# Gated stage of a two-layer hybrid trunk: low halves of weights and operand sums moved from GpSimd to VectorE

## The chip, the cores and the metric

The kernel runs on one core of a Trainium2 chip. The metric is the device time of one execution in microseconds; the median of the runs counts. Engines are named as in the profile: PE (TensorE, matrix products), PEld (its weight loads), DVE (VectorE), ACT (ScalarE), POOL (GpSimd), SP (SyncE, which issues most transfers).

## What is computed

Two layers of a trunk with three parallel branches, over 512 sample tokens and 128 prompt tokens, width 1024, all in fp32. A layer, cut to what matters here:

```python
h = rms_norm(x, norm_g) * (1 + scale) + shift
rq, rk, rv, rz, q_lat, kv_lat, k_r, mz, fu, fz, gl = split(h @ w_in)
o_r = retention(rq, rk, rv); o_m = latent_attention(...); o_f = fourier_mix(fu)
branches = stack([o_r * silu(rz), o_m * silu(mz), o_f * silu(fz)])      # three of width 512
proj = einsum('btnw,nwd->btnd', branches, w_branch)                     # 512 -> 1024 each
merged = sum(proj * sigmoid(gl.reshape(B, T, 3, 1024)), axis=2)
x = x + gate * (merged @ w_out)
```

The gated stage is the part from the last Fourier gates to `merged`: for each of the three branches a product of `h` with 1024 gate columns `gl`, a sigmoid, a product of the branch with its 512 x 1024 matrix, the elementwise product of both, and the sum over branches.

## The kernel before

Activations lie transposed: features on the 128 partitions, 640 tokens (512 + 128) along the free axis, one tile for each 128 features. fp32 products are made from two reduced-precision parts: a value is split into a high half (a cast by ScalarE, `ACT.copy` at L78) and a low half (`low`, L73 and L74: source minus high half, one two-input subtraction on the engine given as `leng`, VectorE by default). A product is then three matmuls, high x high, high x low, low x high (`mm3`, L84 to L87).

A layer runs attention, retention, Fourier mixing, the gated stage and the output projection in turn. In the gated stage every product of a 2 x 2 block structure is made with seven block products instead of eight (`seven`, L1045): the right operand's blocks and the weights' blocks are first summed in certain combinations, then seven products are accumulated in PSUM banks of 320 columns (`bank`, six of them), and each is folded into the two outputs by adds on VectorE that read PSUM (L1052). Per layer:

- 13 gate weight groups of 256 columns (`gl_weights`, L1010): two loads of 512 KB into two `raw` buffers (`wraw`, there are two in all), four sums of 512 columns on VectorE (`wsums`, L1004 to L1008), and splits. The tiles are w1 (1024 columns: the first raw tile as loaded), w2 (two halves of 512: the two sums), w4 (512), and w3 (1024: the first raw tile after the sums changed it in place). Casts of w1 and w3 are at L1015 and L1025. One group (columns `C_FZ + 256`) is for the Fourier gates, 12 are for the branches.
- 12 branch weight groups (`br_weights`, L1031): one load of 512 KB, four sums of 256 columns, and splits of 512, 256, 512 and 512 columns.
- 3 sets of operand sums (`branch_sums`, L975): for each branch seven operand blocks of 2 x 320 columns are split, and four blocks are formed by subtraction or addition.

A raw buffer can be loaded again when its last reader is done; so the casts and low halves that read it, on ScalarE, GpSimd and VectorE, set when the SP queue can issue the next load.

The loop at L1169 goes over the branches (indices 1, 0, 2), and in each over eight steps: an even step makes the gates of 256 columns (`gl_weights`, `seven`), an odd step the branch product (`br_weights`, `seven`), multiplies both (L1203, two inputs, 640 columns) and, from the second branch on, adds the result to the sum `mg` (L1205, 640 columns). The operand sums of the second and third branch are interleaved with the first gate products of that branch. Between the products, matrix products of the conditioning vector (`mod`, L173) are poured in: 12 blocks in layer 0, four in layer 1.

The program is built with a tile framework that inserts the semaphores and plans the order of the instructions on each engine by a timeline of its own (`schedule_with_timeline_sim=True`, L1361); within an engine instructions then run in that fixed order. The order therefore need not be the order of the source: the sums of a branch weight group stand between the PSUM adds of the gate products before it.

In the gated stage before the change the low halves are shared out by hand. In `gl_weights` VectorE makes the first half of w1 and the second sum's half of w2; GpSimd makes the second half of w1, the first sum's half of w2, w4, and w3 in two instructions. In `br_weights` VectorE makes one of 512 columns, GpSimd two of 512 and one of 256. In `branch_sums` GpSimd makes four of seven low halves and one of four sums. Of each two additions at L1205 GpSimd makes one.

Of the kernel before, what the change touches and what calls it, by code (L numbers as in the profile page):

```python
# [11 lines left out]
ALU = mybir.AluOpType  # L12
# [18 lines left out]
def build(nc, tc, A, O):  # L31
    ACT, DVE, POOL, PE = nc.scalar, nc.vector, nc.gpsimd, nc.tensor
# [40 lines left out]
    def low(eng, hi, lo, src):  # L73
        eng.tensor_tensor(lo, src, hi.bitcast(F32), op=ALU.subtract)  # L74

    def split(hi, lo, src, scale=None, leng=DVE):
        if scale is None:
            ACT.copy(hi, src)  # L78
            low(leng, hi, lo, src)
        else:  # L80
            ACT.mul(hi, src, scale)
            DVE.scalar_tensor_tensor(lo, src, scale, hi.bitcast(F32), op0=ALU.mult, op1=ALU.subtract)
# [24 lines left out]
    def rows(w, k0, nk, c0, n):  # L107
        return w[k0 * P:(k0 + nk) * P, c0:c0 + n].rearrange("(k p) n -> p k n", p=P)

# [1 line left out]
    ident = cp.tile([P, P], F32, name="ident")  # L111
    make_identity(nc, ident)
    ones = cp.tile([P, 1], F32, name="ones")
# [20 lines left out]
    vT = cp.tile([P, P], F32, name="vT")  # L134
    DVE.tensor_copy(vT, vps[:, :P])

    # silu of the conditioning vectors
    cs = cp.tile([P, 2 * NK + 30], F32, name="cs")
    DVE.memset(cs, 0.0)
    cth = cp.tile([P, 2, NK], F32, name="cth")  # L140
# [1 line left out]
    DVE.scalar_tensor_tensor(cth, cth, 1.0, cT, op0=ALU.add, op1=ALU.mult)  # L142
    DVE.tensor_scalar(cs[:, 0:2 * NK].rearrange("p (k c) -> p k c", c=2), cth.rearrange("p c k -> p k c"), 0.5, None, op0=ALU.mult)

    # log sigmoid of the decay logits
    ab = cp.tile([P, 16], F32, name="ab")
    DVE.scalar_tensor_tensor(ab, lg, -1.0, lg, op0=ALU.mult, op1=ALU.max)
    ey = cp.tile([P, 16], F32, name="ey")
# [168 lines left out]
                self.pour(24)  # L317
            return self.done[n - 1]

# [1 line left out]
    def lat_mm(acc, t, k, wh, wl, kk):  # L321
        ts_ = slice(t * P, (t + 1) * P)
        return mm3(acc, hh[k][:, ts_], hl[k][:, ts_], wh[:, kk, :], wl[:, kk, :], k == 0, k == NK - 1)
# [4 lines left out]
    def attention(l, ap, w, acc):  # L328
# [35 lines left out]
        for t in order:  # L364
# [2 lines left out]
                lat_mm(a, t, k, *w[k // 3], k % 3)  # L367
            ACT.copy(latv[t], a)
            inv_rms(t, 1, latv[t][:, 0:256], 256)
        # queries  # L370
        wq = []
        for k in range(3):
            rv = wraw(A["w_q_up"][l, k * P:(k + 1) * P, :].unsqueeze(1), 1, 768)
            hi, lo = wtiles(1, 768)
# [24 lines left out]
        mz = Filler(l, [C_MZ + P * w for w in range(4)])  # L399
        mz.finish(1)  # L400

        # keys: normalised latents and rotary parts, both transposed
        nc.sync.dma_start(gkv, A["kv_norm_g"][l].partition_broadcast(P))
        ckh = ap.tile([P, 2, KEYS], F32R, name="ckh")
        ckl = ap.tile([P, 2, KEYS], F32R, name="ckl")
# [28 lines left out]
            POOL.tensor_copy(kth[i][64:96, :], kth[0][64:96, :])  # L434
            POOL.tensor_copy(ktl[i][64:96, :], ktl[0][64:96, :])

        # key/value up-projection weights, nope and value columns apart
        wkv = []
        for k in range(2):
            rv = wraw(A["w_kv_up"][l, k * P:(k + 1) * P, :].unsqueeze(1), 1, 1024)  # L440
            hi, lo = wtiles(1, 1024)
            s = rv.rearrange("p a (h two e) -> p (a two) h e", two=2, e=64)
# [193 lines left out]
                DVE.tensor_tensor(bv[:, :, r], sv[:, :, r], sinv[:, r].unsqueeze(1).to_broadcast([P, nh, 2, 8]), op=ALU.mult)  # L636
        DVE.tensor_tensor(out, a[:, :nh], b[:, :nh], op=ALU.add)

# [1 line left out]
    def retention(l, rp, orr, spare):  # L640
        pos = rp.tile([P, 2, T], F32, name="pos")
        nc.sync.dma_start(pos, A["k_pos"].partition_broadcast(P))
# [169 lines left out]
        norm(3)  # L812
        gate(3)

# [1 line left out]
    def fourier(l, fp, of, sums):  # L816
        def table(name, src, a, n):
            raw = fp.tile([P, a, n], F32, name="traw", tag="traw", bufs=1)
# [111 lines left out]
    def fourier_gate(of, g, z):  # L930
        DVE.scalar_tensor_tensor(of[g], of[g], 0.5, z, op0=ALU.mult, op1=ALU.mult)

# [1 line left out]
    HALF = (slice(0, 320), slice(320, 640))  # L934

    def resplit(hi, lo, eng):
# [38 lines left out]
    def branch_sums(gp, src, spare):  # L975
        sv = src.rearrange("p (i k) n -> p i k n", i=2)
        B = lambda i, c: sv[:, i, :, HALF[c]]
        t = [gp.tile([P, 2, 320], F32R, name=f"bq{i}", tag=f"bq{i}", bufs=1) for i in range(10)]
        x = [spare[:, i, :].rearrange("p (k n) -> p k n", k=2) for i in range(4)]
        t = t[:8] + x[:2] + t[8:] + x[2:]  # L980

        def place(i, x, eng):
            hi, lo = t[2 * i:2 * i + 2]
            split(hi, lo, x, leng=eng)
            return [(hi[:, k, :], lo[:, k, :]) for k in range(2)]

        def run():
            p0 = place(0, B(0, 0), POOL)
            p5 = place(5, B(1, 1), DVE)
            yield p0  # L990
            POOL.tensor_tensor(B(1, 1), B(1, 1), B(0, 1), op=ALU.subtract)
            DVE.tensor_tensor(B(0, 1), B(0, 1), B(0, 0), op=ALU.subtract)
            DVE.tensor_tensor(B(0, 0), B(0, 0), B(1, 1), op=ALU.add)
            yield place(1, B(0, 0), DVE)
            yield place(2, B(1, 0), POOL)
            DVE.tensor_tensor(B(1, 0), B(1, 0), B(0, 0), op=ALU.subtract)
            yield place(3, B(0, 1), DVE)
            yield place(4, B(1, 1), POOL)
            yield p5
            yield place(6, B(1, 0), POOL)  # L1000

        return run()

# [6 lines left out]
    def gl_weights(gp, l, c0):  # L1010
        r1 = wraw(rows(A["w_in"][l], 0, NK, c0, P), NK, P)
        r2 = wraw(rows(A["w_in"][l], 0, NK, c0 + P, P), NK, P)
        lo, up = slice(0, 4), slice(4, 8)
        w1, w2 = wtiles(NK, P), wtiles(NK, P)
        ACT.copy(w1[0], r1)  # L1015
        low(DVE, w1[0][:, lo], w1[1][:, lo], r1[:, lo])
        low(POOL, w1[0][:, up], w1[1][:, up], r1[:, up])
        s1, s2 = (gp.tile([P, 4, P], F32, name="st", tag="st", bufs=2) for _ in range(2))
        wsums(r1[:, lo], r1[:, up], r2[:, lo], r2[:, up], s1, s2)
        split(w2[0][:, up], w2[1][:, up], s2, leng=DVE)  # L1020
        split(w2[0][:, lo], w2[1][:, lo], s1, leng=POOL)
        w4 = [gp.tile([P, 4, P], F32R, name=f"w4{i}", tag=f"w4{i}", bufs=1) for i in range(2)]
        split(w4[0], w4[1], r2[:, up], leng=POOL)
        w3 = wtiles(NK, P)
        ACT.copy(w3[0], r1)  # L1025
        low(POOL, w3[0][:, lo], w3[1][:, lo], r1[:, lo])
        low(POOL, w3[0][:, up], w3[1][:, up], r1[:, up])
        g = lambda w, s: (w[0][:, s], w[1][:, s])
        return g(w1, lo), g(w2, up), g(w1, up), g(w2, lo), g(w3, lo), g(w3, up), w4

    def br_weights(gp, l, idx, c0):  # L1031
        r = wraw(rows(A["w_branch"][l, idx], 0, 4, c0, 256), 4, 256)
        w1, w2 = wtiles(NK, P), wtiles(NK, P)
        c1, c2 = slice(0, P), slice(P, 256)
        s = [slice(2 * i, 2 * i + 2) for i in range(4)]
        split(w1[0][:, 0:4], w1[1][:, 0:4], r[:, :, c1], leng=POOL)
        split(w2[0][:, s[2]], w2[1][:, s[2]], r[:, 2:4, c2], leng=POOL)
        st = gp.tile([P, 4, P], F32, name="st", tag="st", bufs=2)
        wsums(r[:, 0:2, c1], r[:, 2:4, c1], r[:, 0:2, c2], r[:, 2:4, c2], st[:, 0:2], st[:, 2:4])
        split(w1[0][:, 4:8], w1[1][:, 4:8], st, leng=POOL)  # L1040
        split(w2[0][:, 0:4], w2[1][:, 0:4], r[:, :, c1], leng=DVE)
        g = lambda w, i: (w[0][:, s[i]], w[1][:, s[i]])
        return g(w1, 0), g(w1, 3), g(w1, 1), g(w1, 2), g(w2, 0), g(w2, 1), g(w2, 2)
# [23 lines left out]
                add(y2[:, a], y2[:, a])  # L1067
            yield i

# [1 line left out]
    first = []  # L1071

    po1 = sm()
# [45 lines left out]
    for l in range(DEPTH):  # L1119
# [25 lines left out]
        with ExitStack() as s:  # L1145
# [4 lines left out]
            blocks = [(0, b) for b in range(8, 12)] + [(1, b) for b in range(8)] if l == 0 else [(1, b) for b in range(8, 12)]  # L1150
# [18 lines left out]
            for n, (idx, src, tmp) in enumerate(((1, omt, None), (0, ort, om), (2, ort, om))):  # L1169
                parts = branch_sums(gp, src, bql)  # L1170
                bq = [] if n else list(parts)
                for step in range(8):
# [25 lines left out]
                    for st in seven(br_weights(gp, l, idx, 256 * i), bq, *ps):  # L1198
                        if st in (3, 6):
                            next(steps, None)  # L1200
                        if st in (5, 6):
                            y, m, p = y2[st - 5], ms[st - 5], ps[st - 5]
                            DVE.scalar_tensor_tensor(p, y, 1.0, p, op0=ALU.add, op1=ALU.mult)  # L1203
                            if n:
                                (POOL if st == 5 else DVE).tensor_tensor(m, m, p, op=ALU.add)  # L1205
            merge(NK)
        s3.close()
        oft = rp2.tile([P, 4, TT], F32, name="xb", tag="of", bufs=1)
# [156 lines left out]
```

## Time and profile before

| | |
|---|---|
| median of the three runs | 1592.85 us (1592.19 to 1600.37) |
| the profiled execution, span from first to last instruction | 1591.8 us |
| mean granted PE clock | 0.975 |
| gated stage of layer 0, of layer 1 (from the table of windows) | about 442 to 752 us, 1212 to 1516 us |
| busy in the whole span: PE, DVE, ACT, POOL | 1470.8, 1174.7, 740.0, 647.4 us |
| chain that ended last: PE, DVE, issue, DMA, ACT, POOL | 53, 25, 10, 5, 4, 2% |

How to read the rows. In a table of windows each row is one stretch of time: its length, the busy time of each engine with the number of its instructions, the mean granted clock of PE, the share of the DMA engines and GB/s. In a row of the view by source line the three numbers behind the count are the shortest, median and longest duration in ns, then when the first and the last one started, then the shapes. In a view of groups the numbers are the busy time of all, the mean of one, and the idle time of the engine just before them with what ended it. In the timeline a row is start, duration, engine, line, operation, output <- inputs. In the view of waits the three numbers are the time in all, how often, and the longest. L74 is the subtraction that makes a low half, whoever asks for it; the tile names (wl, w, bq, bql) tell them apart. Busy time includes time in which an instruction has begun and is held up.

### The profile page before, as it was taken

How to read it: one execution, taken by the hardware profiler on the slowest of the kernel's cores; microseconds unless marked ns; L12 is line 12 of the kernel's file. 1: busy time of each engine (PE TensorE's matmuls, PEld its weight loads, DVE VectorE, ACT ScalarE, POOL GpSimd, SP SyncE). 2: the span in 40 equal slices, each digit the busy share in tenths (PEclk: the TensorE clock that was granted, in tenths of full speed). 3: DMA queues.
4: the chain of work that ended last, by engine and by line, in shares of the span. 5: the costliest groups of instructions: out<-in, count | busy, mean ns of one | idle time of the engine just before them, and what ended most of it. 6: DMA issues, size and time to landing. Idle time of an engine off the chain costs nothing.

```text
span 1591.8 us, 25637 instructions
## 1 busy us (share of the span) xinstructions
PE 1470.8 (92%) x9713; PEld 1358.5 (85%) x9713; DVE 1174.7 (74%) x1974; ACT 740.0 (46%) x1563; POOL 647.4 (41%) x485
## 2 busy tenths in 40 slices
PE   5999999999889989899999999999988998987997
PEld 3989999979888877788999899998888887887887
DVE  5267775466899899999564777555598899899953
ACT  5456666354444433434254676644344434334332
POOL 1220004444465656665311101164364656575550
PEclk9999999999999999999999999999999999998999
DMA  9320004221134443334532000332122442222342
GB/s 338 121 70 6 10 17 135 74 68 41 48 111 113 121 139 106 93 106 137 159 90 83 15 15 14 100 92 72 37 54 64 136 125 88 67 67 66 84 130 79
DMA packets 174250, 138.93 MB, mean 87 GB/s; under 512 B 8752, under 2 KB 165040, under 8 KB 174128
## 3 DMA queue, kind: packets, MB, share of 16 engines
q1 hardware_dynamic: 172976, 136.94, 29.4%
q8 instruction: 76, 1.25, 0.3%
q10 hardware_dynamic: 1152, 0.37, 0.1%
q14 instruction: 46, 0.38, 0.1%
HBM read 125.98 MB, written 11.30 MB: 86 GB/s over the span
## 4 chain that ended last, share of the span: by engine, by line
PE 53%; DVE 25%; issue 10%; DMA 5%; ACT 4%; POOL 2%; SPq 0%; POOLq 0%; DVEq 0%; ACTq 0%
PE sm L85 5%; PE sm L87 5%; PE sm L86 5%; PE bank L85 4%; PE bank L87 4%; PE bank L86 4%; PE big L491 4%; PE fill L302 3%; PE sm L302 3%; DMA raw<-in_w_in 3%; PE big L253 2%; PE sm L512 2%; DVE wl L74 2%; DVE om L1052 2%; DVE raw L1008 2%
## 5 line engine op out<-in xcount | busy, mean ns | idle before, releaser
L74 POOL TENSOR_TENSOR wl<-raw,wh 128x512 fp32r<-128x512 f32 (+2 forms) x172 | 288.1, 1688 | 456.4 <-ACT wh L78 268.7
L78 ACT CAST wh<-raw 128x512 fp32r<-128x512 f32 (+4 forms) x142 | 109.6, 774 | 170.4 <-DVE raw L1008 56.1
L85 PE MATMUL sm<-wh,hh 128*128 128x256 f32 (+2 forms) x456 | 134.0, 295 | 4.7 <-DVE vl L74 2.3
L85 PE MATMUL bank<-hh,wh 128*128 128x320 f32 x416 | 132.8, 319 | 5.2 <-DVE om L1052 4.5
L87 PE MATMUL sm<-wh,hl 128*128 128x256 f32 (+2 forms) x456 | 132.9, 293 | 2.3 <-DVE hl L74 2.3
L86 PE MATMUL sm<-wl,hh 128*128 128x256 f32 (+2 forms) x456 | 133.3, 292 | 0.0
L86 PE MATMUL bank<-hl,wh 128*128 128x320 f32 x416 | 131.6, 316 | 0.0
L87 PE MATMUL bank<-hh,wl 128*128 128x320 f32 x416 | 130.3, 313 | 0.0
L74 POOL TENSOR_TENSOR wl<-st,wh 128x512 fp32r<-128x512 f32 x50 | 78.3, 1567 | 104.0 <-ACT wh L78 98.9
L78 ACT CAST wh<-st 128x512 fp32r<-128x512 f32 x76 | 47.0, 619 | 158.2 <-DVE st L1005 103.0
L85 PE MATMUL bank<-bq,wh 128*128 128x320 f32 x240 | 80.7, 337 | 16.4 <-ACT om L1054 7.6
L85 PEld LDWEIGHTS sm<-wh,hh 128*128 128x128 f32 x456 | 87.0, 191 | 6.5 <-DVE vl L74 2.7
L74 DVE TENSOR_TENSOR wl<-raw,wh 128x512 fp32r<-128x512 f32 (+4 forms) x74 | 82.2, 1116 | 14.0 <-ACT wh L78 14.0
L85 PEld LDWEIGHTS bank<-hh,wh 128*128 128x128 f32 x416 | 80.0, 192 | 12.9 <-DVE om L1052 8.6
L87 PEld LDWEIGHTS sm<-wh,hl 128*128 128x128 f32 x456 | 86.9, 191 | 3.1 <-DVE hl L74 2.6
L86 PEld LDWEIGHTS sm<-wl,hh 128*128 128x128 f32 x456 | 87.1, 191 | 0.5 <-issue 0.4
L86 PE MATMUL bank<-bq,wh 128*128 128x320 f32 x240 | 78.1, 326 | 8.5 <-DVE bq L74 8.5
L86 PEld LDWEIGHTS bank<-hl,wh 128*128 128x128 f32 x416 | 80.2, 193 | 0.0
L87 PEld LDWEIGHTS bank<-hh,wl 128*128 128x128 f32 x416 | 80.0, 192 | 0.0
L1052 DVE TENSOR_TENSOR om<-bank,om 128x320 f32<-128x320 f32 x168 | 76.7, 481 | 3.5
L74 DVE TENSOR_TENSOR ptl<-sm,pth 128x384 fp32r<-128x384 f32 x128 | 67.3, 549 | 14.1 <-ACT pth L78 13.1
L87 PE MATMUL bank<-bq,wl 128*128 128x320 f32 x240 | 77.6, 323 | 0.0
(571 smaller groups left out, 4945.9 us busy)
## 6 DMA issues: line engine op xcount, KB each, us to landing
raw<-in_w_in SPq DMA_DIRECT2D x96, 512.0 KB, 4.0
mraw<-in_w_mod SPq DMA_DIRECT2D x64, 256.0 KB, 3.9
raw<-in_w_branch SPq DMA_DIRECT2D x24, 512.0 KB, 3.4
raw<-in_w_out SPq DMA_DIRECT2D x16, 512.0 KB, 4.3
mraw<-in_w_mod SPq DMA_DIRECT2D x4, 1024.0 KB, 11.7
mraw<-in_w_mod SPq DMA_DIRECT2D x8, 512.0 KB, 7.9
raw<-in_w_in SPq DMA_DIRECT2D x8, 384.0 KB, 4.5
om<-xd SPq DMA_DIRECT2D x16, 192.0 KB, 3.1
```

Of the source, the lines that this page charges most:

```text
L74: eng.tensor_tensor(lo, src, hi.bitcast(F32), op=ALU.subtract)
L78: ACT.copy(hi, src)
L85: PE.matmul(out, ah, bh, start=first, stop=False)
L86: PE.matmul(out, ah, bl, start=False, stop=False)
L87: return PE.matmul(out, al, bh, start=False, stop=last)
L253: PE.matmul(ps[:, 512 * h:512 * h + 320], ws[a][:, k, :], xs[b][k][:, 320 * h:320 * h + 320], start=(first and k == 0 and i == 0), stop=(l ...
L302: PE.matmul(ps, w[a][:, k, :], (hh, hl)[b][k][:, hs], start=(k == 0 and i == 0), stop=(k == NK - 1 and i == 2))
L491: PE.matmul(S[:, 512 * h:512 * h + 384], qT[hd][a][:, t * P:(t + 1) * P], (kth, ktl)[b][hd % 3][:, 384 * h:384 * h + 384], start=(i == 0), ...
L512: PE.matmul(po[:, :256], vt[hd // 4][kt][:, hd % 4, :], pts[hd, qb][b][kt // 3][:, kt % 3, :], start=(kt == 0 and b == 0), stop=(kt == 5 a ...
L1008: DVE.tensor_tensor(a12, a12, s2, op=ALU.subtract)
L1052: add = lambda o, v: DVE.tensor_tensor(o, ps, v, op=ALU.add)
```

## The change

Low halves and sums of the gated stage move from GpSimd to VectorE, and where a tile's low half was made in two instructions it becomes one:

```diff
 branch_sums:
-            p0 = place(0, B(0, 0), POOL)
+            p0 = place(0, B(0, 0), DVE)
...
-            POOL.tensor_tensor(B(1, 1), B(1, 1), B(0, 1), op=ALU.subtract)
+            DVE.tensor_tensor(B(1, 1), B(1, 1), B(0, 1), op=ALU.subtract)
...
-            yield place(2, B(1, 0), POOL)
+            yield place(2, B(1, 0), DVE)
...
-            yield place(4, B(1, 1), POOL)
+            yield place(4, B(1, 1), DVE)
...
-            yield place(6, B(1, 0), POOL)
+            yield place(6, B(1, 0), DVE)
 gl_weights:
         ACT.copy(w1[0], r1)
-        low(DVE, w1[0][:, lo], w1[1][:, lo], r1[:, lo])
-        low(POOL, w1[0][:, up], w1[1][:, up], r1[:, up])
+        low(DVE, w1[0], w1[1], r1)
...
         ACT.copy(w3[0], r1)
-        low(POOL, w3[0][:, lo], w3[1][:, lo], r1[:, lo])
-        low(POOL, w3[0][:, up], w3[1][:, up], r1[:, up])
+        low(DVE, w3[0], w3[1], r1)
 br_weights:
-        split(w2[0][:, s[2]], w2[1][:, s[2]], r[:, 2:4, c2], leng=POOL)
+        split(w2[0][:, s[2]], w2[1][:, s[2]], r[:, 2:4, c2])
...
-        split(w1[0][:, 4:8], w1[1][:, 4:8], st, leng=POOL)
+        split(w1[0][:, 4:8], w1[1][:, 4:8], st)
 the loop over the branches:
-                                (POOL if st == 5 else DVE).tensor_tensor(m, m, p, op=ALU.add)
+                                DVE.tensor_tensor(m, m, p, op=ALU.add)
```

GpSimd keeps, in `gl_weights`, the low halves of the first sum (part of w2) and of w4, 512 columns each, and in `br_weights` that of the first 512 columns of w1. `hidden_sums` (L940 to L973), which runs in the Fourier stage and uses GpSimd, is not touched. The rest of the diff replaces comment lines by empty ones.

## The prediction

> **What bounds the kernel now.** I read the page first, then the table of windows over the two gated stages, then the same table cut at the places where one weight group follows the next.
>
> ```profile
> PE 1470.8 (92%) x9713; PEld 1358.5 (85%) x9713; DVE 1174.7 (74%) x1974; ACT 740.0 (46%) x1563; POOL 647.4 (41%) x485
> ```
>
> ```profile
> core 0: us, PE busy (x) PEld busy (x) DVE busy (x) ACT busy (x) POOL busy (x), PEclk, DMA share, GB/s
> 442.00:752.00 310.00, 284.66 (x1836) 250.23 (x1834) 284.25 (x387) 120.74 (x201) 185.48 (x121) 0.98 0.40 115
> 1212.00:1516.00 304.00, 269.31 (x1680) 252.19 (x1679) 281.57 (x374) 117.23 (x192) 181.84 (x121) 0.94 0.32 89
> ```
>
> Over the whole program the matrix engine is the bound. In the gated stages (one per layer, together 614 of 1591.8 us) VectorE is as full as PE: 284.25 of 310 us and 281.57 of 304. So the question is which of the two comes last, and where. The next rows cut the stages into pairs: one gate weight group with its seven products, then one branch weight group with its seven.
>
> ```profile
> 521.00:542.60 21.60, 21.60 (x146) 19.37 (x146) 19.27 (x28) 8.30 (x14) 11.23 (x8) 1.00 0.44 124
> 542.60:572.00 29.40, 25.84 (x170) 22.29 (x169) 28.79 (x35) 12.58 (x21) 21.57 (x13) 1.00 0.36 100
> 572.00:594.80 22.80, 22.07 (x145) 19.32 (x146) 20.64 (x31) 8.10 (x14) 13.36 (x9) 1.00 0.55 166
> 594.80:619.10 24.30, 22.38 (x148) 19.39 (x147) 21.31 (x30) 8.19 (x14) 13.78 (x9) 1.00 0.40 114
> 619.10:642.60 23.50, 21.68 (x133) 18.16 (x131) 21.11 (x30) 8.20 (x14) 13.76 (x9) 0.93 0.37 102
> 642.60:673.80 31.20, 26.60 (x166) 23.51 (x165) 30.67 (x36) 12.68 (x21) 23.45 (x14) 0.94 0.33 94
> 673.80:697.10 23.30, 23.30 (x149) 20.34 (x148) 20.62 (x31) 8.11 (x14) 13.28 (x9) 0.93 0.37 105
> 697.10:722.20 25.10, 22.89 (x151) 19.91 (x150) 21.84 (x30) 8.20 (x14) 13.28 (x9) 1.00 0.38 110
> 1314.70:1344.40 29.70, 24.93 (x156) 22.97 (x155) 29.16 (x36) 12.58 (x21) 21.54 (x13) 0.91 0.25 68
> 1367.20:1390.00 22.80, 20.39 (x118) 19.76 (x119) 21.16 (x29) 7.82 (x13) 13.35 (x9) 0.85 0.26 70
> 1390.00:1412.80 22.80, 20.76 (x136) 19.64 (x134) 21.32 (x28) 7.83 (x13) 13.42 (x9) 1.00 0.25 70
> 1412.80:1442.80 30.00, 21.59 (x121) 20.47 (x120) 29.58 (x35) 12.69 (x21) 21.33 (x14) 0.86 0.20 54
> ```
>
> Three kinds of window show. In pairs of the first branch (521.0) PE is busy for 21.60 of 21.60 us at full clock: nothing that frees VectorE shortens them. In pairs of the second and third branch (594.8, 697.1, 1390.0) PE has gaps or a lowered clock, and VectorE is busy all but 1.5 to 3 us. At the change from one branch to the next (542.6, 642.6, 1314.7, 1412.8; I call them transitions) VectorE is full, 29.58 of 30.00, and PE waits. So the change can act in the second and third kind: 12 plain pairs, four transitions, and the two entries of the stages.
>
> **What VectorE's time is made of.** Its busy time is not all work. These rows give smallest, median and largest duration of one instruction in ns, and below them a stretch of both engines' instructions in order of time.
>
> ```profile
> L1052 DVE TENSOR_TENSOR om<-bank,om x168: 472/478/493, 562.3 to 1520.5; 128x320 f32<-128x320 f32 x168
> L1203 DVE SCALAR_TENSOR_TENSOR om<-tg,om x16: 812/1868/2850, 606.0 to 1521.1; 128x640 f32<-128x640 f32 x16
> L74 DVE TENSOR_TENSOR wl<-st,wh x26: 673/679/1776, 447.8 to 1493.9; 128x512 fp32r<-128x512 f32 x26
> L74 DVE TENSOR_TENSOR fw<-ff,fh x16: 408/749/1514, 389.5 to 1194.3; 128x256 fp32r<-128x256 f32 x16
> L1205 DVE TENSOR_TENSOR mg<-mg,om x16: 810/1162/2894, 588.0 to 1522.9; 128x640 f32<-128x640 f32 x16
> L1205 POOL TENSOR_TENSOR mg<-mg,om x16: 1560/2137/2161, 584.8 to 1520.6; 128x640 f32<-128x640 f32 x16
> L74 POOL TENSOR_TENSOR wl<-st,wh x50: 1279/1494/1887, 441.7 to 1499.9; 128x512 fp32r<-128x512 f32 x50
> L74 POOL TENSOR_TENSOR wl<-raw,wh x64: 728/1434/3640, 447.8 to 751.4; 128x512 fp32r<-128x512 f32 x50, 128x256 fp32r<-128x256 f32 x12, 128x1024 fp32r<-128x1024 f32 x2
> ```
>
> ```profile
> 744.28 1.22 DVE L74 TENSOR_TENSOR wl<-raw,wh 128x1024 fp32r<-128x1024 f32 x1
> ```
>
> ```profile
> 1377.33 0.48 DVE L1052 TENSOR_TENSOR om<-bank,om 128x320 f32<-128x320 f32 x1
> 1377.73 3.35 DVE L1203 SCALAR_TENSOR_TENSOR om<-tg,om 128x640 f32<-128x640 f32 x2
> 1381.11 2.09 DVE L1205 TENSOR_TENSOR mg<-mg,om 128x640 f32<-128x640 f32 x1
> ```
>
> ```profile
> 1378.52 1.87 POOL L74 TENSOR_TENSOR wl<-st,wh 128x512 fp32r<-128x512 f32 x1
> 1380.36 2.16 POOL L1205 TENSOR_TENSOR mg<-mg,om 128x640 f32<-128x640 f32 x1
> ```
>
> An add that reads PSUM (L1052) takes 472 to 493 ns whatever goes on. An instruction with both inputs in SBUF takes 0.81 us at best (L1203) and 1.87 in the median. From 1377.73 on two of them took 3.35 us and the next 2.09, while GpSimd was in its own two-input instructions without a break. So the two engines take turns at SBUF: each GpSimd instruction that meets such a VectorE instruction holds it up. The smallest durations are what the work costs alone: VectorE 0.67 us for 512 columns, 0.41 for 256, 0.81 for 640, 1.22 for 1024; GpSimd 1.28, 0.73 (the least of its mixed row), and 1.56. The same work costs GpSimd nearly twice as long, and the time is partly charged to VectorE.
>
> The Trainium skill (SBUF — State Buffer, section "Who interferes with whom") states this as an exclusive lock: the one that comes second waits for the whole instruction of the first, and VectorE instructions with one SBUF input are exempt. The trace agrees in the exemption (472 to 493 ns). By that rule alone every microsecond left on GpSimd that meets a two-input VectorE instruction is a full stop, which would be the low end of the gain worked out below.
>
> **The sum, for one pair.** I take the window at 1390.0, with 28 VectorE instructions in 21.32 us. Work alone: 14 adds at 0.48 (6.7), six of 512 columns (4.0), four of 256 and one of 512 (2.3), three of 640 (2.4): 15.5 us. Each starts 0.08 before the last one ends (the add at 1377.33 lasts 0.48, the next starts after 0.40), so 28 x 0.08 = 2.2 comes off: 13.3. The other 8.0 us are stalls. GpSimd's nine instructions there cost alone 7 x 1.28 + 0.73 + 1.56 = 11.25. Stall per microsecond of GpSimd work: 8.0 / 11.25 = 0.71.
>
> The change, in this pair. Off GpSimd: three low halves of 512 columns of the gate group, one of 512 and one of 256 of the branch group, one sum of 640: 4 x 1.28 + 0.73 + 1.56 = 7.41; three of 1.28 stay, 3.84. Onto VectorE: two of 1024 columns in place of one of 512 (2.44 - 0.67), one of 512, one of 256, one of 640: 3.66, less four more overlaps of 0.08, so 3.3. VectorE's work becomes 16.6. For the stalls from the remaining 3.84 us the ends are 0.71 of it as now (2.7) and all of it (3.84), since VectorE will have fewer moments in which a GpSimd instruction harms nobody; I take 0.85, 3.3 us. VectorE: 13.3 + 8.0 = 21.3 now, 16.6 + 3.3 = 19.9 after; gain 1.4 us (0.8 with full stalls, 2.0 at 0.71).
>
> **All places.** Plain pairs in layer 0: PE was full at 21.6 there, so the pair at 572.0 gives at most 1.2; the other four shown and the last one, which looks alike, 1.4 each: 8.2. Layer 1, six pairs: 8.4. In the four transitions the same 1.4, and the operand sums of the next branch: four low halves and one subtraction of 640 leave GpSimd (7.8 us, of which 0.71, so 5.5, stalled VectorE) and cost VectorE 5 x 0.81 - 0.4 = 3.65: 1.9 more, 3.3 each, 13.2 together. The two entries have these sums as well, partly beside the end of the Fourier stage: 1 each, between 0 and 3.3. Pairs of the first branch: nothing, as long as PE stays covered; VectorE had 2.3 us to spare at 521.0 and its load falls there too. Removed labels and comments cost nothing. The sums of hidden columns (L951, L954 and the GpSimd halves around them) are not in the diff, so the Fourier stage stays as it is.
>
> Sum: 8.2 + 8.4 + 13.2 + 2 = 31.8 us off the profiled span of 1591.8, 1560.0. The median of the runs lies 1.05 above that span, so I predict 1561.0.
>
> What the moves put in a queue. VectorE takes its instructions in order; the low halves of the first and third gate tiles now wait there for ScalarE's cast, and behind them wait the adds that empty PSUM. The rows that bear on it:
>
> ```profile
> L74 DVE TENSOR_TENSOR wl<-raw,wh 128x512 fp32r<-128x512 f32 x24 | 27.6, 1154 | 0.3 <-ACT wh L78 0.3
> L1005 DVE TENSOR_TENSOR st<-raw 128x512 f32<-128x512 f32 x12 | 8.6, 719 | 18.2 <-DMA raw<-in_w_in 18.2
> ```
>
> ```profile
> L1015 ACT CAST wh<-raw x26: 1040/1044/1051, 408.5 to 1483.5; 128x1024 fp32r<-128x1024 f32 x26
> ```
>
> ```profile
> 1371.71 0.37 SPq L92 DMA_DIRECT2D raw<-in_w_branch  x1
> ```
>
> VectorE already runs one low half behind the cast of L1015 and idled 0.3 us in all for it, so I cost the wait at nothing; without that cover it is up to 1.04 us each time. GpSimd keeps the low half of the fourth gate tile, whose end lets the branch weights be loaded (the issue at 1371.71). It may now stand behind a VectorE instruction of 1.22 us: 0 to 1.2 us later per pair, and less when GpSimd no longer has a backlog; I take 0.
>
> **Rivals.** *The loads set the pace.* VectorE idled 18.2 us in layer 0 for the gate weights alone. There are two raw buffers, so gate and branch loads follow one another, and if freeing the buffers does not get earlier, the time that VectorE saves turns into longer idle time before L1005. For it: the idle time stands in nearly every plain pair. Against it: part of what frees a buffer is VectorE's own chain, which gets shorter, and the transitions are full without such idle time. Then only the transitions gain, 0 to 13 us: 1580 to 1593.
>
> *A larger gain.* If the three remaining GpSimd instructions fall mostly beside PSUM adds, with stalls of 0.3 x 3.84 = 1.15, a pair gains 3.5. Layer 0, stopped by PE at 21.6, gives 14; layer 1 gives 21; transitions 4 x 5.4 = 22; entries 4: 61 us, 1531. The lowered clock helps this rival.
>
> ```profile
> PE bank L85 <- DVE tg L1052: 7.3, 7, 1.8
> PE bank L85 <- ACT bq L78: 6.0, 2, 4.4
> PE bank L87 <- DVE wl L74: 4.6, 1, 4.6
> ```
>
> These waits of PE in layer 1 go with a mean clock of 0.94 against 0.98 in layer 0, or 18 us of lost PE time in 304. The Trainium skill (TensorE: Matmul & The Clock Gate, section "HAM oscillation — how this bites in real kernels") says that idle stretches of over 3.4 us drop PE to half rate; two of the waits above are that long, and by that rule shortening them would return a part of the 18 us.
>
> *Slower: the casts block VectorE's queue.* If the low halves of the first and third gate tiles stand at the head of VectorE's queue until their casts end, the adds behind them wait, PSUM banks stay taken and PE stops, also in the pairs where it is now full. At 1.04 us each, twice in 26 gate groups, that costs 54 us; less the 32 gained, 1591.8 + 22 = 1614. It decides from about 0.6 us a time. Against it: the 0.3 us above. For it: in the first-branch pairs PE has no slack at all. That the order on each engine is planned anew when the program is built can bring this about.
>
> **Chances.** Forecast, 1545 to 1577: 0.50. Larger gain: 0.18. Loads set the pace, or half of it, 1577 to 1595: 0.21. Slower: 0.11. About 0.5%, 8 us, is what a measurement of this kernel can tell from no change. Faster by more than that (under 1585): 0.50 + 0.18 + about half of the third, 0.79. Same: 0.10. Slower: 0.11. The range 1530 to 1595 leaves out the slower rival and the far end of the larger gain.
>
> **What would show it.** In the changed profile GpSimd should be busy some 55 to 65 us in each gated stage instead of 185; the median of L1203 should fall from 1.87 to under 1.2; plain pairs in layer 1 should last 21 to 22 us, transitions 26 to 28, first-branch pairs 21.5 as now; VectorE's busy time in a stage should fall by 10 to 25 us though its instructions become more. I am wrong if VectorE's two-input instructions stay stretched, if its idle time before L1005 grows by what the stalls lose, or if PE shows new waits on L1052 in the first-branch pairs.

## The result, and the profile after

The changed kernel takes 1546.17 us (median, 1542.11 to 1552.12) beside 1592.52 us (1591.96 to 1600.37) for the kernel before in the same measurement: a ratio of 0.969, 95% interval 0.967 to 0.9709. The forecast was 1561.0, with a range of 1530 to 1595. The profiled execution of after has a span of 1542.3 us (before 1591.8). In after the lines behind `gl_weights` have numbers two smaller: the PSUM adds are L1050 (L1052 before), the products of gates and branches L1201, the additions L1203.

The page's first part, whole program:

```profile
PE 1452.5 (94%) x9713; PEld 1349.5 (87%) x9713; DVE 1133.2 (73%) x2094; ACT 746.2 (48%) x1563; POOL 395.8 (26%) x313
```

VectorE has 120 instructions more than before and is busy 41.5 us less; GpSimd is busy 251.6 us less. The table of windows over the two gated stages:

```profile
core 0: us, PE busy (x) PEld busy (x) DVE busy (x) ACT busy (x) POOL busy (x), PEclk, DMA share, GB/s
440.00:725.00 285.00, 275.99 (x1839) 248.87 (x1838) 263.38 (x442) 119.36 (x197) 57.13 (x37) 0.99 0.44 125
1188.00:1471.00 283.00, 259.07 (x1677) 244.40 (x1676) 262.71 (x434) 119.38 (x191) 66.56 (x37) 0.97 0.34 96
```

Set against the rows of before: the stages are 25 and 21 us shorter, VectorE is busy 20.9 and 18.9 us less in them, GpSimd 128 and 115 us less, and PE's clock rose from 0.98 to 0.99 and from 0.94 to 0.97. From the first to the last product that fills a PSUM bank the stages take 284.7 and 283.0 us (before 309.4 and 303.5): 45.2 of the 49.5 us by which the span shrank. The same table by pairs, cut at the first sum of each gate group as before:

```profile
515.30:535.90 20.60, 20.60 (x140) 18.18 (x138) 18.52 (x32) 8.40 (x14) 3.89 (x3) 1.00 0.48 129
535.90:561.70 25.80, 25.80 (x173) 22.45 (x171) 25.77 (x42) 13.47 (x22) 5.23 (x4) 1.00 0.38 104
561.70:586.30 24.60, 24.60 (x166) 21.48 (x164) 21.02 (x40) 10.35 (x18) 4.85 (x3) 1.00 0.56 170
586.30:607.80 21.50, 21.50 (x150) 20.09 (x146) 18.87 (x32) 7.79 (x13) 5.00 (x3) 1.00 0.42 123
607.80:628.90 21.10, 21.10 (x143) 18.86 (x143) 19.18 (x33) 7.36 (x12) 4.45 (x3) 1.00 0.45 124
628.90:653.50 24.60, 21.87 (x150) 18.29 (x149) 24.57 (x41) 12.66 (x22) 6.72 (x4) 1.00 0.42 119
1333.60:1354.60 21.00, 19.30 (x132) 19.04 (x131) 18.63 (x30) 8.20 (x13) 4.26 (x3) 1.00 0.28 76
1375.90:1403.60 27.70, 23.14 (x141) 21.88 (x140) 26.95 (x44) 11.36 (x18) 8.87 (x3) 0.94 0.21 58
1425.40:1446.20 20.80, 20.80 (x143) 20.80 (x143) 18.86 (x33) 8.26 (x13) 4.40 (x3) 1.00 0.28 76
```

In layer 0 PE now fills the plain pairs of the second branch (561.7, 586.3, 607.8): 21.10 of 21.10 us at full clock. Of the four transitions two (628.9, 1375.9) are still VectorE's; in the first of each stage (535.9 is shown) both engines are full. In layer 1 the last plain pair cut here (1425.4) is full of PE, but in others (1333.6) neither engine is full: VectorE is busy 18.63 of 21.00 us. What it waits for stands in the groups by line; first two rows of before, which the prediction did not show, then those of after (the last columns: idle time before these instructions, and what ended it):

```profile
L1005 DVE TENSOR_TENSOR st<-raw 128x256 f32<-128x256 f32 x24 | 19.9, 827 | 4.1 <-DMA raw<-in_w_branch 4.0
L1005 DVE TENSOR_TENSOR st<-raw 128x512 f32<-128x512 f32 x26 | 19.7, 757 | 34.1 <-DMA raw<-in_w_in 34.1
```

```profile
L74 DVE TENSOR_TENSOR wl<-raw,wh 128x1024 fp32r<-128x1024 f32 x62 | 75.7, 1224 | 4.3 <-ACT wh L78 1.6 <-ACT wh L1024 1.4 <-ACT wh L1015 1.3
L1005 DVE TENSOR_TENSOR st<-raw 128x512 f32<-128x512 f32 x26 | 18.2, 699 | 23.9 <-DMA raw<-in_w_in 23.9
```

VectorE still stands idle for 23.9 us because gate weights have not arrived. The moved low halves of 1024 columns cost 1.22 us each, as forecast, and waited 1.4 + 1.3 us in all for the two casts of `gl_weights`.

The instructions that were stretched before, by line:

```profile
L1201 DVE SCALAR_TENSOR_TENSOR om<-tg,om x16: 807/812/3012, 594.3 to 1471.8; 128x640 f32<-128x640 f32 x16
```

The median is 0.81 us (before 1.87); the longest is still 3.01. One stretch of after's timeline shows both sides of what is left:

```profile
1384.29 0.81 DVE L1201 SCALAR_TENSOR_TENSOR om<-tg,om 128x640 f32<-128x640 f32 x1
...
1386.50 0.81 DVE L1203 TENSOR_TENSOR mg<-mg,om 128x640 f32<-128x640 f32 x1
1386.71 5.77 POOL L74 TENSOR_TENSOR wl<-raw,wh 128x512 fp32r<-128x512 f32 x1 [6.97 <-ACT wh L78]
1387.23 1.21 DVE L74 TENSOR_TENSOR wl<-raw,wh 128x1024 fp32r<-128x1024 f32 x1
...
1391.25 0.48 DVE L1050 TENSOR_TENSOR om<-bank,om 128x320 f32<-128x320 f32 x1
1391.65 1.12 DVE L1006 TENSOR_TENSOR st<-st,raw 128x256 f32<-128x256 f32 x1
...
1398.90 0.68 DVE L74 TENSOR_TENSOR wl<-raw,wh 128x512 fp32r<-128x512 f32 x1
1399.50 3.46 DVE L1050 TENSOR_TENSOR om<-bank,om 128x320 f32<-128x320 f32 x8
1399.64 0.37 SPq L92 DMA_DIRECT2D raw<-in_w_in  x1
1403.60 0.69 DVE L1005 TENSOR_TENSOR st<-raw 128x512 f32<-128x512 f32 x1 [0.64 <-DMA raw<-in_w_in]
```

A GpSimd instruction that costs 1.28 us alone takes 5.77, since VectorE has a row of two-input instructions without a gap; it gets in when VectorE reads PSUM (1391.25), and then holds up the next two-input instruction a little (1.12 instead of 0.41 at 1391.65). Further down: VectorE's last low half from a raw buffer ends at 1399.58, the load into that buffer is issued at 1399.64, and VectorE meets the data at 1403.60. So VectorE's own work is part of the loop that feeds it.

### The profile page after: what moved, and what is told of

The parts are those of the page before. It is cut to its first block, busy times and chain, and to the rows that moved or that the text cites. A ratio compares the mean times of both kernels' runs of the same rounds, so it can differ in the third digit from the quotient of the medians.

```text
span 1542.3 us, 25448 instructions
## 1 busy us (share of the span) xinstructions
PE 1452.5 (94%) x9713; PEld 1349.5 (87%) x9713; DVE 1133.2 (73%) x2094; ACT 746.2 (48%) x1563; POOL 395.8 (26%) x313
## 3 DMA queue, kind: packets, MB, share of 16 engines
q1 hardware_dynamic: 172976, 136.94, 30.3%
## 4 chain that ended last, share of the span: by engine, by line
PE 59%; DVE 21%; DMA 8%; issue 7%; ACT 4%; POOL 1%; SPq 1%; POOLq 0%; ACTq 0%; DVEq 0%
PE bank L85 5%; PE sm L85 5%; PE sm L87 5%; PE sm L86 5%; PE bank L86 5%; PE bank L87 5%; DMA raw<-in_w_in 5%; PE big L491 4%; PE fill L302 3%; DVE wl L74 3%; PE sm L302 3%; PE sm L512 2%; PE big L253 2%; PE fill L181 2%; PE sm L504 2%
## 5 line engine op out<-in xcount | busy, mean ns | idle before, releaser
L74 POOL TENSOR_TENSOR wl<-raw,wh 128x1024 fp32r<-128x1024 f32 (+1 forms) x70 | 158.4, 2265 | 480.7 <-ACT wh L78 365.5
L74 DVE TENSOR_TENSOR wl<-raw,wh 128x1024 fp32r<-128x1024 f32 (+4 forms) x124 | 117.7, 961 | 16.7 <-ACT wh L78 14.0
L74 POOL TENSOR_TENSOR w<-raw,w 128x512 fp32r<-128x512 f32 x26 | 39.7, 1525 | 209.0 <-ACT w L78 163.1
L85 PE MATMUL bank<-bq,wh 128*128 128x320 f32 x240 | 77.0, 323 | 3.5 <-ACT om L1052 2.2
L1050 DVE TENSOR_TENSOR om<-bank,om 128x320 f32<-128x320 f32 x168 | 75.0, 478 | 6.1 <-PE bank L87 5.5
L74 DVE TENSOR_TENSOR ptl<-sm,pth 128x384 fp32r<-128x384 f32 x128 | 67.3, 549 | 14.1 <-ACT pth L78 12.9
L87 PE MATMUL bank<-bq,wl 128*128 128x320 f32 x240 | 73.9, 312 | 1.0 <-DVE wl L74 0.8
L86 PE MATMUL bank<-bq,wh 128*128 128x320 f32 x240 | 74.6, 311 | 0.0
```

Of the source, the lines that this page charges most:

```text
L85: PE.matmul(out, ah, bh, start=first, stop=False)
L86: PE.matmul(out, ah, bl, start=False, stop=False)
L87: return PE.matmul(out, al, bh, start=False, stop=last)
L1050: add = lambda o, v: DVE.tensor_tensor(o, ps, v, op=ALU.add)
```

## The experiments

**The theory** was that of the prediction (A): VectorE paces the stage, and what the change brings is the loss of stalls that GpSimd's two-input instructions cause in VectorE's. **Rivals**: that it is GpSimd's occupation as such, whatever it does there; that it is the wider instructions; that the loads through two raw buffers set the pace. A stall is counted here as the duration of a VectorE instruction less the short end (5th percentile) of the same form, summed over a stage; stages run from the first to the last product that fills a PSUM bank. The kernels ran on several chips, and each ratio is to runs of the kernel before on the same chip (medians of 1592.52 to 1596.28 us), so it can differ a little from the quotient of two medians of the table. Stages and stalls are those of one profiled execution.

| kernel | median us | ratio to before, 95% interval | gated stages us | stalls us |
|---|---|---|---|---|
| before | 1592.52 | 1 | 309.4, 303.5 | 96.2, 94.9 |
| after | 1546.17 | 0.969 (0.967 to 0.9709) | 284.7, 283.0 | 32.3, 29.5 |
| idle two-input work on GpSimd | 1605.4 | 1.0049 (1.0032 to 1.0065) | 312.1, 316.4 | 62.2, 65.1 |
| idle fills on GpSimd | 1544.23 | 0.9675 (0.9657 to 0.9692) | 286.2, 280.0 | 32.0, 27.3 |
| no low half left on GpSimd | 1547.91 | 0.9695 (0.9678 to 0.9711) | 295.7, 279.2 | 5.0, 3.8 |
| 1024 columns in two | 1549.27 | 0.9697 (0.9677 to 0.9716) | 292.3, 287.9 | 30.8, 31.5 |
| before + gate part | 1581.22 | 0.992 (0.99 to 0.994) | 304.5, 302.5 | 71.9, 71.0 |
| before + branch part | 1585.85 | 0.9947 (0.9925 to 0.9968) | 306.3, 300.5 | 74.8, 75.3 |
| before + operand part | 1567.96 | 0.9833 (0.9818 to 0.9847) | 296.8, 295.5 | 70.8, 75.2 |
| after, no second gate load | 1523.41 | 0.9555 (0.9541 to 0.9569) | 279.8, 268.9 | 31.8, 29.6 |
| after + third buffer | 1515.84 | 0.9501 (0.9483 to 0.9519) | 279.4, 266.8 | 30.3, 30.3 |
| after + its small tiles only | 1551.38 | 0.9731 (0.9707 to 0.9755) | 290.8, 283.5 | 29.6, 28.3 |
| before + third buffer | 1555.87 | 0.9752 (0.9727 to 0.9776) | 291.6, 283.3 | 84.0, 82.0 |
| before + its small tiles only | 1615.51 | 1.0129 (1.0105 to 1.0152) | 321.3, 312.3 | 83.9, 88.7 |

Outside the gated stages the profiled executions take between 968 and 982 us, in no order that I can explain; so a difference of a few microseconds in the median, or in one stage, says little by itself.

**Idle two-input work, idle fills.** Both kernels are after, with GpSimd work that nobody waits for, on a tile of its own: four instructions behind the low half of the first gate sum, and two behind that of the branch weights.

```diff
+        with tc.issue_after(i.ins):
+            for _ in range(4):
+                POOL.tensor_tensor(dummy[0], dummy[0], dummy[0], op=ALU.mult)
```

The other kernel has `POOL.memset(dummy[0], 0.0)` there, 8 and 4 times.

> The changed kernel plus GpSimd subtractions-in-kind that nobody waits for: after the low half that GpSimd keeps in each gate group four, and in each branch group two, two-input instructions of 384 columns on a spare tile (the outputs are unchanged). VectorE's own work is that of the changed kernel. Theory A (the gain comes from VectorE no longer being held up at SBUF by GpSimd's two-input instructions; measured 0.62 us of stall per us of GpSimd work before, 0.61 to 0.67 after): about 5.9 us of GpSimd work more per pair, 3.7 us more stall, PE runs out of cover in all pairs: 1590 to 1610, VectorE's instructions with two SBUF inputs stretched again (median of L1201 well over 1 us). Theory B (the gain comes from the low halves and sums being done sooner on an engine that is twice as fast, and VectorE's stalls only fill time): nothing waits for the added work but the fourth tile's low half behind it: 1546 to 1556.

> As the kernel with idle two-input instructions, at the same places in GpSimd's queue, but the added instructions are fills of 384 columns, eight after a gate group's low half and four after a branch group's, which read nothing from SBUF. Theory A with the collision at the reading side: no added stalls, 1544 to 1556, VectorE's two-input instructions at their shortest. If every GpSimd instruction collides, or if GpSimd's being busy is what matters (its fourth tile's low half comes later): as the other one, 1580 to 1610.

By tile, and by windows, for the two-input work and then for the fills:

```profile
L1025 POOL TENSOR_TENSOR dm<-dm x104: 825/1268/1853, 437.8 to 1505.7; 128x384 f32<-128x384 f32 x104
L1040 POOL TENSOR_TENSOR dm<-dm x48: 823/1052/1692, 468.2 to 1510.2; 128x384 f32<-128x384 f32 x48
L1210 DVE SCALAR_TENSOR_TENSOR om<-tg,om x16: 809/1444/3028, 604.1 to 1530.4; 128x640 f32<-128x640 f32 x16
```

```profile
438.00:750.00 312.00, 283.19 (x1836) 252.30 (x1835) 293.58 (x443) 120.63 (x200) 146.99 (x114) 0.97 0.40 114
1211.00:1528.00 317.00, 269.64 (x1680) 252.02 (x1679) 298.24 (x435) 118.75 (x192) 150.03 (x114) 0.95 0.30 86
```

```profile
L1025 POOL MEMSET dm<- x208: 407/418/429, 439.1 to 1452.6; 128x384 f32 x104
```

```profile
439.00:726.00 287.00, 275.54 (x1841) 248.32 (x1840) 263.90 (x442) 119.66 (x198) 119.32 (x190) 0.99 0.43 124
1189.00:1470.00 281.00, 258.50 (x1682) 244.91 (x1682) 260.78 (x435) 118.70 (x191) 129.56 (x190) 0.98 0.34 96
```

GpSimd is busy about 120 to 130 us in a stage with the fills and about 150 with the two-input work. The fills leave VectorE's busy time at 264 and 261 us and the time where it was; the two-input work raises it to 294 and 298 us and takes the whole gain back. The median product of gates and branches (here L1210) goes from 0.81 to 1.44 us, as theory A had it. VectorE's instructions are as many as in after (one more or less at the edge of a window). The stages grow by 27.4 and 33.4 us, VectorE's stalls by 29.9 and 35.6: here a stall went almost one for one into the time. GpSimd's occupation as such falls as a cause: with the fills it is nearly as occupied, and nothing gets slower. That the collision is one of reading is what the Trainium skill (SBUF — State Buffer, section "Who interferes with whom") states: a VectorE instruction with two SBUF inputs contends with a GpSimd instruction that reads SBUF, not with one that only writes it. These two runs agree, at 0.42 us a fill without effect.

**No low half left on GpSimd, and narrow ones.**

```diff
-        split(w2[0][:, lo], w2[1][:, lo], s1, leng=POOL)
+        split(w2[0][:, lo], w2[1][:, lo], s1, leng=DVE)
...
-        split(w4[0], w4[1], r2[:, up], leng=POOL)
+        split(w4[0], w4[1], r2[:, up], leng=DVE)
...
-        split(w1[0][:, 0:4], w1[1][:, 0:4], r[:, :, c1], leng=POOL)
+        split(w1[0][:, 0:4], w1[1][:, 0:4], r[:, :, c1], leng=DVE)
```

> The three low halves per pair that the change leaves on GpSimd go to VectorE too: no GpSimd instruction of any size is left inside the gated stage. Theory A: VectorE's work grows by 3 x 0.68 - 0.24 = 1.8 us per pair, its stalls of about 2.4 us per pair go: 0.6 us per pair less, 1535 to 1550, VectorE's two-input instructions all at their shortest. Theory B: the fourth tile's low half frees its raw buffer earlier, so a little faster as well; but if VectorE's load by count is the bound, 1.8 us on 24 pairs: 1575 to 1590.

```profile
438.00:734.00 296.00, 277.51 (x1839) 249.68 (x1838) 257.75 (x478) 123.38 (x200) 4.34 (x2) 0.98 0.42 121
1190.00:1470.00 280.00, 257.34 (x1682) 241.68 (x1681) 256.58 (x469) 119.84 (x192) 1.77 (x1) 0.99 0.35 97
```

```profile
L1005 DVE TENSOR_TENSOR st<-raw 128x256 f32<-128x256 f32 x24 | 10.0, 416 | 7.5 <-DMA raw<-in_w_branch 7.5
```

The stalls are nearly gone (5.0 and 3.8 us, 27.3 and 25.7 less than in after), some 35 instructions a stage more stand on VectorE, about 25 us of work by their short ends, and its busy time falls only 6 us below after's. The time is that of after. So the change stops near the balance: the last three low halves cost about as much on one engine as on the other. What VectorE saved was not turned into time: in the profiled execution the stage of layer 0 is 11.0 us longer than in after although VectorE is busy 5.6 us less in it. VectorE idles 16.5 us more there: 7.0 of these for branch weights (the row above), 5.1 for PE, 3.2 for ScalarE's cast of L1015.

```diff
-        low(DVE, w1[0], w1[1], r1)
+        low(DVE, w1[0][:, lo], w1[1][:, lo], r1[:, lo])
+        low(DVE, w1[0][:, up], w1[1][:, up], r1[:, up])
```

(and the same for w3.)

> The changed kernel with each instruction of 1024 columns split in two of 512 again, all on VectorE. Shortest durations 2 x 0.67 against 1.22, less one overlap of 0.08: 0.05 to 0.12 us more for each of 52 instructions: 3 to 6 us, 1549 to 1553. If the width of the instructions carries the gain (fewer handovers between the engines): half of the gain lost, 1565 to 1575.

1549.27 us, 3 above after's median, with overlapping intervals: by the medians the width of the instructions cannot be told from no effect. In the one profiled execution the stages are 7.6 and 4.9 us longer than after's, so the width may carry up to about a quarter of the gain, not half of it.

**One part at a time**: the kernel before with the gate lines of the diff alone, the branch lines alone, and the operand sums with the addition at L1205 alone.

> The kernel before with the gate groups' part of the change alone (w1 and w3 in one instruction each on VectorE). Theory A (VectorE's stalls): GpSimd loses 3.84 us per pair, VectorE gains 1.7 us of work and loses 0.62 x 3.84 = 2.4 us of stall: 0.7 us per pair where VectorE is last, about 16 of 24: 1575 to 1585. Theory B (results come sooner): w3's low half frees the first raw buffer, so most of the gain: 1555 to 1568.

> The kernel before with the branch groups' part alone (one low half of 512 and one of 256 columns on VectorE). Theory A: GpSimd loses 2.0 us per pair, VectorE gains 0.93 of work and loses 1.25 of stall: 0.3 us per pair: 1584 to 1592. Theory B: these tiles stand at the end of GpSimd's backlog in front of the branch products: 1570 to 1580.

> The kernel before with the operand sums' part alone (branch_sums and the additions at L1205). Theory A: 0.3 us per pair of the second and third branch, 1.9 us in each of four transitions and up to 3 in the two entries, plus shorter chains of low halves there: 1570 to 1582. Theory B: only the transitions and entries: 1575 to 1585. If the three parts add up to the whole gain of 46 us, the parts are independent; if they give clearly less than the whole together, the last GpSimd work to go is worth the most.

The ratios lie 0.8, 0.5 and 1.7% below one, together 3.0%; the whole change 3.1%. The parts add up, and each takes 20 to 25 us of stalls out of a stage. The gate and the branch part came out in A's ranges and outside B's. The operand part brought 2 us more than A allowed; it is the largest, as it also frees the transitions and entries, where VectorE was fullest.

**The loads.** After still idles 23.9 us for gate weights, so I took away the second of the two loads of a group:

```diff
-        r2 = wraw(rows(A["w_in"][l], 0, NK, c0 + P, P), NK, P)
+        r2lo, r2up = keep[-1][:, :, 0:P].bitcast(F32), keep[-1][:, :, P:256].bitcast(F32)
```

> The changed kernel without the second load of each gate group: its operand is taken from a tile that lies in SBUF all through the stage, so half of the gate weights are left out. If the loads through two raw buffers now set the pace (PE in layer 1 waits 13.1 us for ScalarE's cast of the second sum, which waits for that load): 15 to 30 us off, 1517 to 1531, and that wait goes. If PE or VectorE is last even so: 1538 to 1548.

1523.41 us: the loads hold up what is left in after. Another way is to give the second load a buffer of its own; to make room the sums are formed in the raw tiles (s2 in place of r2's lower half), and the tiles for sums and for conditioning weights become fewer:

```diff
-        r2 = wraw(rows(A["w_in"][l], 0, NK, c0 + P, P), NK, P)
+        r2 = gp.tile([P, NK, P], F32, name="raw3", tag="raw3", bufs=1)
+        nc.sync.dma_start(r2, rows(A["w_in"][l], 0, NK, c0 + P, P))
...
-        wsums(r1[:, lo], r1[:, up], r2[:, lo], r2[:, up], s1, s2)
+        DVE.tensor_tensor(s1, r2[:, lo], r2[:, up], op=ALU.add)
+        DVE.tensor_tensor(r1[:, lo], r1[:, lo], r2[:, lo], op=ALU.subtract)
+        DVE.tensor_tensor(s2, r2[:, up], r1[:, lo], op=ALU.subtract)
+        DVE.tensor_tensor(r1[:, up], r1[:, up], s2, op=ALU.subtract)
```

> The changed kernel with a buffer of its own for the second load of each gate group, so that three loads can be under way. To make room, the second sum is formed in place of the half of the second raw tile that is no longer needed (as upper half minus the already changed half of the first tile, the same value by another order of the subtractions), one sum tile instead of two, and two buffers for the conditioning weights instead of three. If the loads set the pace of the changed kernel, this gets a good part of what leaving the load out gave (22 us): 1525 to 1538. If the smaller tiles cost as much as the buffer gives, or the wait is for something else: 1542 to 1555.

> The control for the third buffer: the changed kernel with its smaller tiles and the sum in place, but with two raw buffers as before. Raw tile two is now held until the second sum is split, and there is one sum tile less: 1546 to 1560. If it is as fast as the one with the third buffer, the buffer does nothing.

The first sum of a gate group and the windows, with the third buffer; then the same sum with the small tiles alone:

```profile
L1019 DVE TENSOR_TENSOR st<-raw 128x512 f32<-128x512 f32 x26 | 19.8, 763 | 0.2 <-DMA raw<-in_w_in 0.2
```

```profile
440.00:720.00 280.00, 276.81 (x1838) 247.98 (x1837) 263.74 (x446) 124.52 (x203) 60.33 (x39) 0.99 0.45 128
1175.00:1442.00 267.00, 254.32 (x1677) 241.40 (x1677) 260.95 (x433) 120.77 (x194) 67.67 (x39) 0.98 0.36 101
```

```profile
L1018 DVE TENSOR_TENSOR st<-raw 128x512 f32<-128x512 f32 x26 | 17.9, 689 | 30.2 <-DMA raw<-in_w_in 30.1
```

1515.84 us, 9 below what I expected at best, and the fastest of all kernels here: 5% under before. On the same chip the small tiles alone gave 1551.38, so the buffer is worth 35.5 us beside them. The wait for gate weights is gone. What bounds the stages now can be read in the windows: PE in layer 0 (276.81 of 280), VectorE in layer 1 (260.95 of 267).

Would the kernel before have had this gain too? I expected little, since its VectorE looked full.

> The kernel before with the same smaller tiles and the third buffer. If VectorE, held up by GpSimd, was the bound there and the loads were not, the buffer gives little: 1583 to 1597. If the loads set the pace before the change as well: 1565 to 1577.

> The kernel before with the smaller tiles of the run before (one tile for the sums instead of two, the second sum formed in place of the second raw tile, two tiles for the conditioning weights) but with the two raw buffers that it has: the control for the kernel before with a third buffer (1555.87 us, 0.9752). Theory A, the third buffer itself made that gain, by taking away the 34.1 us that VectorE idled for the gate weights: the small tiles alone change little, 1588 to 1604 us, and the idle time before the first sum stays above 30 us. Rival, the gain came from the smaller tiles or from the other form of the sums (fewer instructions that read two tiles): 1556 to 1578 us here as well, with the idle time as before. A time between, 1578 to 1588, would mean that both have a share.

The first expectation missed: 1555.87 us. The control missed as well, on the other side: the small tiles alone make the kernel before slower, 1615.51 us. Beside them the buffer is worth 60 us there; some 20 of these only undo what the small tiles cost, and the two together gain 40. The sums in each, third buffer first:

```profile
L1020 DVE TENSOR_TENSOR st<-raw 128x512 f32<-128x512 f32 x26 | 19.2, 740 | 0.5
```

```profile
L1019 DVE TENSOR_TENSOR st<-raw 128x512 f32<-128x512 f32 x26 | 19.3, 741 | 35.4 <-DMA raw<-in_w_in 35.4
L1005 DVE TENSOR_TENSOR st<-raw 128x256 f32<-128x256 f32 x24 | 15.7, 655 | 36.6 <-DMA raw<-in_w_branch 29.5 <-POOL wl L74 7.1
```

Without the buffer the idle time for the gate weights stays at 35.4 us, and with the small tiles (a single tile for the sums, and the second raw tile held until the second sum is split) another 36.6 us appear before the branch sums, 29.5 of them for branch weights, where before has 4.1. My mistake was to take "VectorE is full" for a bound that excludes another. In before VectorE was busy 284 of 310 us, and the wait for loads was most of the rest: stage time is the busy time plus those waits, one behind the other. The change shortens the first, a buffer the second, and the two nearly multiply: 0.969 x 0.9752 = 0.945, against 0.9501 with both. The split is not that clean in the kernel before: with small tiles and buffer its VectorE is also busy less,

```profile
440.00:732.00 292.00, 281.13 (x1830) 249.30 (x1828) 275.28 (x387) 121.81 (x201) 183.88 (x122) 0.98 0.43 123
1192.00:1475.00 283.00, 259.51 (x1675) 242.24 (x1674) 270.05 (x373) 117.66 (x193) 183.16 (x121) 0.97 0.34 95
```

that is 9 and 11.5 us of the 18 and 21 by which these windows are shorter. The stalls there are 12.2 and 12.9 us lower than in before, and the small tiles alone already lower them by 12.3 and 6.2; so about half of that gain is not the wait for loads.

## Why the prediction was right, and what in it was off

The direction and mechanism held: VectorE's two-input instructions are held up by GpSimd's, and taking these away is worth more than the work that VectorE takes over. The forecast gain was 31.8 us of the span; 49.5 came, and the median lies at the fast edge of the 1545 to 1577 us to which I gave even odds. Point by point:

- **VectorE's work and busy time.** The instructions alone rose by 50.5 us in a stage (211.9 to 262.4, summing the short ends of their forms), and the stalls fell by 63.9 and 65.4. Busy time fell by 20.9 and 18.9, in the forecast 10 to 25. That is more than the 13 to 15 us between the two, in the main because some 57 instructions more also overlap more: at 0.08 us each about 4.5 us, an estimate. GpSimd's 57.13 us lie in the 55 to 65, its 66.56 just above, and the median 0.81 under the 1.2.
- **The mis-sized term: 0.85 us of stall for each microsecond left on GpSimd.** I raised it above the 0.71 of one window because fewer harmless moments would be left. Over whole stages it was 0.63 and 0.62 before (96.2 and 94.9 over 152.7 us of GpSimd work alone) and 0.66 and 0.61 after (32.3 and 29.5 over 48.6). It did not rise; and taking the last 48.6 us of it away, with no low half left on GpSimd, removed 0.56 and 0.53 us of stall for each. With 0.64 the remaining 3.84 us of a pair stall VectorE for 2.5 us in place of 3.3.
- **Where the gain fell.** Cut at the first gate sums, the four transitions gained 16.3 us (120.2 to 103.9; forecast 13.2, and three of them are shorter than the 26 to 28 us that I named), the ten plain pairs between them 12.0 (233.1 to 221.1; forecast 13.8), the last pairs of the two stages 6.8 (forecast 2.8), and the entries with the first branch 9.7 (forecast 2). The sum is the stages' 45. So the plain pairs came out near the forecast in part by luck, as two errors met: the stalls fell further, but PE closed the pairs of layer 0 (21.50 of 21.50 us and its neighbours), and in layer 1 VectorE was left with idle time (18.63 of 21.00). The ends of the stages were set too low, the entries above all: "1 each, between 0 and 3.3" was 4.4 and 5.3 by VectorE's sums, and 2.6 and 2.8 up to PE's last product of the first branch, which VectorE runs ahead of.
- **First-branch pairs gain nothing.** The products of such a pair (14.3 and 7.7 us in the trace of both kernels) take 22.0 us before and after.
- **The wait behind the casts, costed at nothing.** 2.7 us in all for both casts over 52 low halves, 0.05 us a time; the rival that ended slower needed 0.6.
- **The release of the raw buffers, costed at 0 to 1.2 us later.** It can be far later, as the 5.77 us instruction shows. Still the idle time before L1005 fell from 34.1 to 23.9 us. That VectorE's own part of the chain got shorter is only argued: with 1024 columns in two, at almost the same work, it was 31.8.
- **The rival "the loads set the pace"** expected that idle time to eat the gain. It fell instead, so this rival was wrong for the change. But the wait itself was real, before and after, and larger than I priced it (18.2 us of one layer): with the third buffer it is gone, and 35 us of time with it.
- **The rival "a larger gain"** had 0.3 of stall per microsecond, which no stage showed; yet what it said of the clock came true in part. PE's busy time fell by 8.7 and 10.2 us for nearly the same instructions, with the clock at 0.99 and 0.97. Whether the clock shortened the stage or only followed the shorter waits, these runs don't separate.
- **A new wait of PE.** PE's waits in layer 1 for VectorE's PSUM adds shrank (those on `tg` from 7.3 us, L1052, to 0.5, L1050; those on `om` from 6.9 to 1.2). In their place, in after's second stage:

```profile
PE bank L85 <- ACT wh L78: 13.1, 5, 4.7
PE bank L87 <- DVE wl L74: 5.3, 3, 3.1
```

PE waits for ScalarE's cast of weights, and that cast for the data. With the third buffer the first of these falls to 5.0 us in two waits.

## What to carry to other kernels

Busy time of VectorE may be mostly waiting: compare the median of each two-input form with its shortest, and where they differ by a factor of two while GpSimd works on SBUF, moving GpSimd's work to VectorE can make VectorE less busy. Price the stall by the average over the whole stage, not by one window. When an engine looks full, read also what ends its remaining idle time: stage time is the busy time plus those waits, and a buffer that removes them can be worth nearly as much as the faster work. Test the smaller tiles that make room for a buffer alone as well: here they cost time.

## What the runs showed of the hardware

- Two-input GpSimd work cost VectorE 0.61 to 0.66 us of stall for each microsecond in the stages of before and after, by GpSimd's shortest durations. The idle work, 76 instructions of 0.82 us in a stage or 62.5 us alone, added 29.9 and 35.6 us, 0.48 and 0.57; held up itself, it was busy for 89.7 and 92.1 us. Why the price is somewhat less, smaller instructions or their place, stays open.
- GpSimd instructions that only write (0.42 us for 384 columns) cost VectorE nothing.
- The hold works both ways: a GpSimd instruction of 1.28 us took 5.77 in a row of VectorE's two-input instructions, and it delays whoever waits for the buffer that it reads.
